# Turning the FFNs' token-major tall-set tiles with VectorE block transposes and ScalarE band copies instead of TensorE transposes, with six temporaries instead of nine

## The chip, the cores and the metric

The kernel runs on one core of one Trainium2 chip. The metric is the device time of one execution in microseconds (us), the median of several runs. TensorE (PE) multiplies matrices, VectorE (DVE) and ScalarE (ACT) work on tiles elementwise, GpSimd (POOL) issues only DMAs here, and SyncE (SP) issues the weight loads. Each engine runs its own instructions in order; they meet at semaphores.

## The reference, cut to what matters

One block of a model with 512 tokens of width 1024, in fp32: a feed-forward network (FFN), a mixer (short convolution and gated linear attention), a second FFN, and a last norm. The change touches the two FFNs only.

```
def swiglu(x, w_gu, w_down):                       # x: 512 x 1024, w_gu: 1024 x 5632
    g, u = jnp.split(x @ w_gu, 2, axis=-1)         # g, u: 512 x 2816
    return (jax.nn.silu(g) * u) @ w_down           # w_down: 2816 x 1024

x = x + 0.5 * swiglu(rmsnorm(x, g1), ffn1_w_gu, ffn1_w_down)
x = x + hybrid_mixer(rmsnorm(x, gm), ...)
x = x + 0.5 * swiglu(rmsnorm(x, g2), ffn2_w_gu, ffn2_w_down)
return rmsnorm(x, gf)
```

## The kernel before, in words

**Products.** Every fp32 product is made of three passes: each operand is split into a rounded high part and a remainder, and PE adds high x high, high x low and low x high. For weights, ACT casts the loaded tile `f` to `wh` (line 382) and DVE forms `wl = f - wh` (line 383). Activations are split the same way into `op` tiles (lines 673 and 674). There are three `wh` and three `wl` buffers, and a weight step is cast two steps ahead of the step that PE works on (`W.take`, `W.issue`).

**Seven products for eight.** Most large products are done by a Strassen-like scheme with seven block products, called m1, p2, q6, p5, q7, p3 and p4. It needs sums of weight blocks (accumulating DMAs on POOL, line 349, and a DVE subtraction for q7, line 376) and sums of operand blocks (lines 653 to 660).

**Tall sets.** The hidden width is 2816 = 22 tiles of 128, held in `hid` as [128 partitions, 22 tiles, 512 tokens]: hidden unit on the partitions, token along the row. Most of `hid` is made by *tall sets* (`up_tall`), each of four tiles starting at tile `f`. FFN 1 has four of them (f = 4, 8, 12, 16) and FFN 2 five (f = 0, 6, 10, 14, 18); the other tiles come from one ordinary set in each FFN, and from a plain start in FFN 1. A tall set has 14 steps: each of the seven products in two halves of the contraction. One step is 12 matmuls of 128x128 by 128x512 (line 701) and one pair `wh`, `wl`. In a tall set the activations are the stationary operand, so its results come out *token-major*: token on the partitions, hidden unit along the row, in PSUM banks `mm`. ACT and DVE combine them in temporaries `tp` of 128x512 (allocated with `T()`): g for the first 256 tokens after m1, p2 and p4, u after p5 and q7, and the second 256 tokens after q6 and p3. At the end of a set four `tp` tiles hold silu(g)·u for the four blocks of 128 tokens.

**The turn.** Since `hid` must have the hidden unit on the partitions, each set's four tiles are turned during the set behind it. `turn(f, js)` does two of the four `hid` tiles: for each it lets PE make four 128x128 fp32 transposes against `ident` into a PSUM tile `aux` (line 845) and ACT copies `aux` to `hid` (line 847). It is called twice for every set, by hooks after the next set's last m1 step and after the first half of its second product.

**What sets the order.** PE's order is the order in which the code is written (`manual_schedule`). The other engines' instructions are placed by a scheduler from the written order and its own estimates. Tile pools track reuse: a `tp` tile is given again when all its readers are done. In FFN 2 the hooks of the tall sets also hold the transposes of `X` (`natural`, line 1069) and, from the last set (f = 18) on, the splits of `hid` for the down projection (`make`).

Of the kernel before, what the change touches and what calls it, by code (L numbers as in the profile page):

```python
# [15 lines left out]
P = 128  # L16
S = 512
# [10 lines left out]
NTB = S // P  # L28
# [77 lines left out]
STEPS = []  # L106
# [28 lines left out]
TALL = {}  # L135
# [44 lines left out]
UPS = {}  # L180
# [54 lines left out]
def block_kernel(ctx: ExitStack, tc: tile.TileContext, xT, vecs, gf, gup, wgl, wts, out):  # L235
    nc = tc.nc
# [12 lines left out]
    def phase(odd, **bufs):  # L249

        stack = ExitStack()
        for n, b in bufs.items():
            pools[n] = stack.enter_context(
                tc.tile_pool(name=n if n != "small" else odd, bufs=b, reuse_waits="tile"))
        return stack

    def tile_of(pool, shape, dtype=F32):
        cnt[0] += 1
        return pools[pool].tile(shape, dtype, tag=pool, name=f"{pool}{cnt[0]}")

    def T(dtype=F32):
        return tile_of("tp", [P, S], dtype)
# [5 lines left out]
    def AUX():  # L268
        cnt[0] += 1
        return pa.tile([P, S], F32, tag="aux", name=f"aux{cnt[0]}")  # L270
# [133 lines left out]
    W = Weights(2)  # L404

    ident = front.tile([P, P], F32, tag="ident", name="ident")
# [180 lines left out]
    def mul(out_, a, b, eng=None):  # L587
        (eng or nc.vector).tensor_tensor(out=out_, in0=a, in1=b, op=ALU.mult)
# [201 lines left out]
    def ffn(up, down, norm, nxt, plain, at):  # L790
        hid = tile_of("hid", [P, KF, S])
        xo = begin_plain(up, hid, norm, plain, at) if plain else begin_weighed(hid, norm)

        def root(t):
            return 1.0 if plain else norm.r[t]

        def minus(t):
            return -1.0 if plain else norm.minus[t]

        done_tiles = {}  # L800

        def up_tall(f):
            g, u = {}, {}

            def done(p, banks):
                for t in range(2):
                    b = banks[t]
                    if p == "m1":
                        g[t] = T()
                        nc.scalar.copy(g[t], b)  # L810
                    if p == "p2":
                        nc.vector.tensor_tensor(out=g[t], in0=b, in1=g[t], op=ALU.add)
                        nc.scalar.activation(g[t], g[t], AF.Silu, scale=root(t))
                    if p == "p5":
                        u[t] = T()
                        nc.scalar.activation(u[t], b, AF.Copy, scale=-1.0)
                    if p == "q6":
                        g[2 + t] = T()
                        nc.scalar.copy(g[2 + t], b)  # L819
                    if p == "q7":  # L820
                        nc.vector.scalar_tensor_tensor(out=u[t], in0=b, scalar=-1.0, in1=u[t],
                                                       op0=ALU.mult, op1=ALU.add)
                    if p == "p3":
                        nc.vector.tensor_tensor(out=g[2 + t], in0=b, in1=g[2 + t], op=ALU.add)
                        nc.scalar.activation(g[2 + t], g[2 + t], AF.Silu, scale=root(2 + t))
                        if plain:
                            mul(u[t], u[t], g[2 + t])
                        else:
                            nc.vector.scalar_tensor_tensor(
                                out=u[t], in0=u[t], scalar=root(2 + t), in1=g[2 + t],  # L830
                                op0=ALU.mult, op1=ALU.mult)
                    if p == "p4":
                        nc.vector.scalar_tensor_tensor(out=g[t], in0=b, scalar=minus(t),
                                                       in1=g[t], op0=ALU.mult, op1=ALU.mult)
                if p == "p4":
                    done_tiles[f] = [g[0], g[1], u[0], u[1]]

            return Tall(xo, done)

        def turn(f, js):  # L840

            for j in js:
                o = AUX()
                for t in range(NTB):
                    nc.tensor.transpose(o[:, t * P : (t + 1) * P],  # L845
                                        done_tiles[f][t][:, j * P : (j + 1) * P], ident)
                nc.scalar.copy(hid[:, f + j], o)

        def up_set(i):
            f = [f for kind, f in UPS[up] if kind == "set"][i]  # L850
# [26 lines left out]
        def turn_pair(f):  # L877

            for j in range(2):
                o = AUX()  # L880
                for t in range(NTB):
                    c = (t % 2) * HW + j * P
                    nc.tensor.transpose(o[:, t * P : (t + 1) * P], narrow[t // 2][:, c : c + P],
                                        ident)
                nc.scalar.copy(hid[:, f + j], o)
# [39 lines left out]
        def at_step(key, f):  # L925
            hooks.setdefault(key, []).append(f)
# [27 lines left out]
        def begin(i):  # L954
            kind, f = UPS[up][i]
            return [((up, f), 1, "m1"), ((up, f), 0, ORDERS[up, f][1])] if kind == "tall" else \
                [(0, "q6"), (0, "p5")]

        if not plain:
            at_step(((up, UPS[up][0][1]), 1, "p5"), norm.finish)  # L960
        count = 0
        for i, (kind, f) in enumerate(UPS[up]):
            if kind == "set":
                if not plain:
                    at_step(begin(i + 1)[0], lambda f=f: turn_pair(f))
                continue
            keys = (begin(i + 1) if i + 1 < len(UPS[up]) else
                    [((down, 0), 1, "m1"), ((down, 0), 0, "p2")])
            for key, js in zip(keys, ((0, 1), (2, 3))):
                at_step(key, lambda f=f, js=js: turn(f, js))  # L970
            if nxt is None and i > 0:
                for p in ("p5", "q7"):
                    at_step(((up, f), 1, p), lambda i=count: natural(i))
                    count += 1
        hls = []
        if nxt is None:
            f = UPS[up][-1][1]
# [22 lines left out]
        def all_banks():  # L1000
            return [AUX(), AUX()] + [MM() for _ in range(KD - 2)]
# [15 lines left out]
        o = all_banks()  # L1017
# [36 lines left out]
        o = all_banks()  # L1054
# [9 lines left out]
    def natural(i):  # L1064

        X = XS[-1]
        o = AUX()
        for t in range(NTB):
            nc.tensor.transpose(o[:, t * P : (t + 1) * P], X[:, i, t * P : (t + 1) * P], ident)
        nc.scalar.copy(X[:, i], o)  # L1070
# [676 lines left out]
        for d, o in [(d, mm_single("w_o", KD, d * P, m_h, m_l)) for d in range(KD - 2, KD)]:  # L1747
            evac(d, o)

    FFN = dict(hid=1, tp=9)  # L1750
    with phase("small1", **FFN):
        W.phase(1)
        n1 = Norm(V_G1)
        for k in range(KD):
            nc.sync.dma_start(x[k], xT[k])
            if k == 0:
                with tc.manual_schedule(engines={ENG.DVE}):
                    n1.part(0, sooner=True)
                    W.issue()
            if k == 1 or k == 3:  # L1760
                W.issue()
        W.early = 5
        for k in range(KD):
            n1.add(k)
        nm = Norm(V_GM)
        ffn("ffn1_w_gu", "ffn1_w_down", n1, nm, PLAIN1, 5)
    with phase("small2", v=4, qk=2, g=1, y=1, small=1, tp=6):
        W.phase(4, 5)
        n2 = Columns(V_G2)
        mixer(nm, n2)  # L1770
    with phase("small3", **FFN):
        W.phase(5)
        ffn("ffn2_w_gu", "ffn2_w_down", n2, None, PLAIN2, 5)
# [43 lines left out]
```

## Time and profile before

| | |
|---|---|
| time, median of 3 runs | 1166.73 us (1166.69 to 1167.82) |
| span of the profiled execution, first to last instruction | 1165.7 us |
| PE busy | 1158.1 us (99%), 6428 matmuls |
| DVE busy | 895.6 us (77%) |
| ACT busy | 658.1 us (56%) |
| POOL busy | 127.3 us (11%) |
| mean granted TensorE clock | 0.999 |

The time of the profiled execution by itself is not given; its span is 1.0 us below the median time, which is taken as what lies around the span. Busy time is the union of an engine's instructions. Matmuls overlap in the records: each lasts longer than the distance to the next one, so a matmul's cost on PE's path is read from starts, or from the chain of work that ended last, and not from its mean duration.

### The profile page before, as it was taken

To read this page: it belongs to the slowest core of one execution; us is meant where nothing else is said; L and a number is where in the kernel's file an instruction comes from. 1 tells how busy PE (TensorE), PEld (TensorE's weight loads), DVE (VectorE), ACT (ScalarE), POOL (GpSimd) and SP (SyncE) were. 2 spreads that over 40 slices of the span, in tenths; PEclk is the share of its full clock that TensorE was granted. 3 is DMA by queue.
4 is the path that set the end of the run, shared out by engine and by line. 5 is a ranking of instruction groups with operands and counts; after the bars stand their busy time and mean duration, and the time that the engine had idled before them with its cause. 6 is when DMAs were issued, how large, how long until landed. Compare 5 with 4: busy or idle time off the path is not lost.

```text
span 1165.7 us, 16523 instructions
## 1 busy us (share of the span) xinstructions
PE 1158.1 (99%) x6428; PEld 1010.7 (87%) x6428; DVE 895.6 (77%) x1066; ACT 658.1 (56%) x832; POOL 127.3 (11%) x167
## 2 busy tenths in 40 slices
PE   9999999999999999999999999999999999999997
PEld 8888888989988888889999998888888888888886
DVE  7985666889887976777797999556876666799966
ACT  6565555634452756575655577525755556575543
POOL 0101110001120110111110111000111101101100
PEclk9999999999999999999999999999999999999999
DMA  9577786657665485878576787834567877877711
GB/s 365 130 187 163 167 219 163 174 131 174 170 206 152 99 220 155 219 198 216 134 175 163 177 215 213 287 104 126 118 181 163 219 181 163 210 168 173 184 41 73
DMA packets 59870, 203.22 MB, mean 174 GB/s; under 512 B 6960, under 2 KB 7088, under 8 KB 59792
## 3 DMA queue, kind: packets, MB, share of 16 engines
q0 software_dynamic: 20288, 73.41, 33.5%
q1 hardware_dynamic: 36912, 124.27, 32.7%
q10 hardware_dynamic: 2592, 4.49, 1.0%
q8 instruction: 50, 0.82, 0.3%
q14 instruction: 28, 0.23, 0.1%
HBM read 124.55 MB, written 8.39 MB: 114 GB/s over the span
## 4 chain that ended last, share of the span: by engine, by line
PE 99%; DVE 1%; ACT 0%; issue 0%; POOL 0%; POOLq 0%
PE mm L701 49%; PE mm L618 24%; PE mm L437 6%; PE mm L415 3%; PE mm L414 3%; PE mm L413 3%; PE aux L845 1%; PE mm L456 1%; PE mm L455 1%; PE mm L454 1%; PE mm L1088 1%; PE mm L1086 1%; PE mm L1087 1%; PE aux L1432 1%; PE aux L1435 0%; PE aux L1415 0%
## 5 line engine op out<-in xcount | busy, mean ns | idle before, releaser
L382 ACT CAST wh<-f 128x1024 fp32r<-128x1024 f32 (+1 forms) x349 | 365.2, 1048 | 358.7 <-PE mm L701 135.8
L383 DVE TENSOR_TENSOR wl<-f,wh 128x1024 fp32r<-128x1024 f32 (+1 forms) x349 | 424.6, 1218 | 177.0 <-ACT wh L382 176.1
L701 PE MATMUL mm<-wh,op 128*128 128x512 f32 x1680 | 528.3, 391 | 0.0
L701 PEld LDWEIGHTS mm<-wh,op 128*128 128x128 f32 x1680 | 315.4, 188 | 65.6 <-ACT tp L819 0.8
L701 PE MATMUL mm<-wl,op 128*128 128x512 f32 x840 | 327.3, 390 | 0.1
L618 PE MATMUL mm<-op,wh 128*128 128x256 f32 x1456 | 263.5, 284 | 0.0
L618 PEld LDWEIGHTS mm<-op,wh 128*128 128x128 f32 x1456 | 227.3, 192 | 0.7
L349 POOL DMA_DIRECT2D f<-f x132 | 113.8, 862 | 907.6 <-DVE wl L383 336.8
L618 PE MATMUL mm<-op,wl 128*128 128x256 f32 x728 | 206.0, 283 | 0.0
L701 PEld LDWEIGHTS mm<-wl,op 128*128 128x128 f32 x840 | 157.8, 188 | 32.5 <-DVE wl L383 0.9
L618 PEld LDWEIGHTS mm<-op,wl 128*128 128x128 f32 x728 | 139.4, 191 | 0.0
L673 ACT CAST op<-hid 128x1024 fp32r<-128x1024 f32 x42 | 44.0, 1050 | 22.5 <-PE mm L701 11.2
L674 DVE TENSOR_TENSOR op<-hid,op 128x1024 fp32r<-128x1024 f32 x42 | 51.2, 1220 | 3.0 <-ACT op L673 2.9
L413 PE MATMUL mm<-op,wh 128*128 128x512 f32 x132 | 51.4, 389 | 0.0
L414 PE MATMUL mm<-op,wh 128*128 128x512 f32 x132 | 51.4, 389 | 0.0
L415 PE MATMUL mm<-op,wl 128*128 128x512 f32 x132 | 51.4, 389 | 0.0
L437 PE MATMUL mm<-op,wh 128*128 128x512 f32 x192 | 48.2, 392 | 0.0
L376 DVE TENSOR_TENSOR f<-f,f 128x1024 f32<-128x1024 f32 x30 | 36.6, 1221 | 12.4 <-DMA f<-f 10.2
L437 PEld LDWEIGHTS mm<-op,wh 128*128 128x128 f32 x192 | 35.7, 188 | 8.0 <-ACT wh L382 0.5
L413 PEld LDWEIGHTS mm<-op,wh 128*128 128x128 f32 x132 | 24.8, 188 | 5.2
L414 PEld LDWEIGHTS mm<-op,wh 128*128 128x128 f32 x132 | 24.8, 188 | 5.2
L415 PEld LDWEIGHTS mm<-op,wl 128*128 128x128 f32 x132 | 24.8, 188 | 5.1
(326 smaller groups left out, 1196.4 us busy)
## 6 DMA issues: line engine op xcount, KB each, us to landing
f<-wts SPq DMA_DIRECT2D x219, 512.0 KB, 4.3
f<-f POOLq DMA_DIRECT2D x132, 512.0 KB, 5.2
X<-xT SPq DMA_DIRECT2D x8, 256.0 KB, 5.7
xs<-X POOLq DMA_DIRECT2D x8, 256.0 KB, 2.8
ga<-tp ACTq DMA_DIRECT2D x8, 256.0 KB, 5.2
gb<-tp ACTq DMA_DIRECT2D x8, 256.0 KB, 4.1
tp<-ga SPq DMA_DIRECT2D x8, 256.0 KB, 4.5
X<-xs POOLq DMA_DIRECT2D x8, 256.0 KB, 7.3
```

What stands on the lines that cost most here:

```text
L349: nc.gpsimd.dma_start(out_, a, accum_op=ALU.add)
L376: nc.vector.tensor_tensor(out=a11, in0=a11, in1=a22, op=ALU.subtract)
L382: nc.scalar.copy(h[:, :w], raw[:, :w])
L383: nc.vector.tensor_tensor(out=l[:, :w], in0=raw[:, :w], in1=h[:, :w].bitcast(F32), op=ALU.subtract)
L413: nc.tensor.matmul(o, wh, ah, start=first, stop=False)
L414: nc.tensor.matmul(o, wh, al, start=False, stop=False)
L415: nc.tensor.matmul(o, wl, ah, start=False, stop=last)
L437: nc.tensor.matmul(o[c], w[:, s : s + P], a[k], start=k == 0 and j == 0, stop=k == kt - 1 and j == 2)
L618: nc.tensor.matmul(to, ww[:, s], aa[:, t], start=fresh and k == 0 and e == 0 and j == 0, stop=k == 3 and j == 2, skip_group_check=True)
L673: nc.scalar.copy(hv, v)
L674: nc.vector.tensor_tensor(out=lv, in0=v, in1=hv.bitcast(F32), op=ALU.subtract)
L701: nc.tensor.matmul(self.bank[b][e], aa[:, c], ww, start=fresh and i == 0 and n == 0, stop=k == 3 and n == 2, skip_group_check=True)
```

## The change

In a tall set, when a pair of final tiles is ready (u after p3, g after p4), DVE transposes each of them blockwise, every 32x32 block by itself, into a new tile `z` of [128, 4 token blocks, 512]. In `z` the values inside a block are where they belong, and the blocks are still in the wrong partition bands. ACT puts them right: `move` copies, for each of the 4 source bands and 4 destination bands of 32 partitions, 32 partitions x 512 values from `z` to `hid`; that is 16 copies for a set. They are hooked onto the 12 steps behind the set (`after`), spread evenly. PE makes no transposes for the tall sets any more. The pool of `tp` tiles has six buffers instead of nine, and there is one `z` buffer, of the size of four `tp` tiles.

```diff
                 if p == "p4":
                     ...
+                if p == "p3":
+                    zs[f] = tile_of("z", [P, NTB, S])
+                    for t in range(2):
+                        block_turn(zs[f], 2 + t, u[t])
                 if p == "p4":
-                    done_tiles[f] = [g[0], g[1], u[0], u[1]]
+                    for t in range(2):
+                        block_turn(zs[f], t, g[t])
 
-        def turn(f, js):
-            for j in js:
-                o = AUX()
-                for t in range(NTB):
-                    nc.tensor.transpose(o[:, t * P : (t + 1) * P],
-                                        done_tiles[f][t][:, j * P : (j + 1) * P], ident)
-                nc.scalar.copy(hid[:, f + j], o)
+        def block_turn(z, at, v):
+            nc.vector.transpose(z[:, at], v)
+
+        def move(z, f, a, q):
+            src = z[32 * a : 32 * (a + 1)].rearrange("p t (b r) -> p b t r", r=P)
+            dst = hid[32 * q : 32 * (q + 1), f : f + 4].rearrange("p b (t r) -> p b t r", r=P)
+            nc.scalar.copy(dst[:, :, :, 32 * a : 32 * (a + 1)], src[:, :, :, 32 * q : 32 * (q + 1)])
 ...
+        def after(i):
+            seq, n = [], W.taken
+            while STEPS[n][1] is not None:
+                seq.append(STEPS[n])
+                n += 1
+            ups = [j for j, (n_, _) in enumerate(seq)
+                   if n_ in TALL and TALL[n_][0] == (up, UPS[up][i][1])]
+            at = max(ups) + 1
+            keys = []
+            for n_, p_ in seq[at : at + 12]:
+                keys.append((*TALL[n_], p_) if n_ in TALL else (0, p_))
+            return keys
 ...
-            keys = (begin(i + 1) if i + 1 < len(UPS[up]) else
-                    [((down, 0), 1, "m1"), ((down, 0), 0, "p2")])
-            for key, js in zip(keys, ((0, 1), (2, 3))):
-                at_step(key, lambda f=f, js=js: turn(f, js))
+            quads = [(a, q) for a in range(4) for q in range(4)]
+            keys = after(i)
+            for n, (a, q) in enumerate(quads):
+                at_step(keys[n * len(keys) // 16], lambda f=f, a=a, q=q: move(zs[f], f, a, q))
 ...
-    FFN = dict(hid=1, tp=9)
+    FFN = dict(hid=1, tp=6, z=1)
```

How the instructions stand on the engines, at three places. Names are those of the tiles, `out<-in`, with the size written; `x3` means three in a row. Lines of the changed kernel are some 20 higher than those of before from here on.

**ScalarE, first steps of FFN 1's third tall set (f = 12).** Line 810 evacuates m1, line 813 is the silu after p2. Before:

```order
L382 CAST wh_1463<-f_1362 128x1024
L810 COPY tp_1480<-mm_1444 128x512
L810 COPY tp_1482<-mm_1445 128x512
L847 COPY hid_193<-aux_1484 128x512
L847 COPY hid_193<-aux_1490 128x512
L382 CAST wh_1498<-f_1318 128x1024
L382 CAST wh_1526<-f_1360 128x1024
L847 COPY hid_193<-aux_1514 128x512
L847 COPY hid_193<-aux_1520 128x512
L382 CAST wh_1554<-f_1322 128x1024
```

After, at the same place:

```order
L382 CAST wh_1467<-f_1357 128x1024
L853 COPY hid_196<-z_1403 32x16x32 x3
L810 COPY tp_1484<-mm_1446 128x512
L810 COPY tp_1486<-mm_1447 128x512
L382 CAST wh_1491<-f_1310 128x1024
L853 COPY hid_196<-z_1403 32x16x32 x2
L382 CAST wh_1508<-f_1355 128x1024
L853 COPY hid_196<-z_1403 32x16x32 x4
L382 CAST wh_1538<-f_1314 128x1024
```

Three band copies now stand ahead of m1's evacuations, two and four ahead of the two following weight casts, where two pairs of copies from PSUM stood.

**VectorE, the same place.** Line 833 makes the last g tiles of the set before (f = 8), line 376 is the weight subtraction for q7, line 812 the addition after p2. Before:

```order
L833 SCALAR_TENSOR_TENSOR tp_1178<-mm_1141,tp_1178 128x512
L383 TENSOR_TENSOR wl_1447<-f_1320,wh_1446 128x1024
L383 TENSOR_TENSOR wl_1464<-f_1362,wh_1463 128x1024
L383 TENSOR_TENSOR wl_1499<-f_1318,wh_1498 128x1024
L376 TENSOR_TENSOR f_1318<-f_1318,f_1324 128x1024
L383 TENSOR_TENSOR wl_1527<-f_1360,wh_1526 128x1024
L376 TENSOR_TENSOR f_1360<-f_1360,f_1366 128x1024
L812 TENSOR_TENSOR tp_1480<-mm_1496,tp_1480 128x512
L812 TENSOR_TENSOR tp_1482<-mm_1497,tp_1482 128x512
L383 TENSOR_TENSOR wl_1555<-f_1322,wh_1554 128x1024
```

After:

```order
L833 SCALAR_TENSOR_TENSOR tp_1185<-mm_1146,tp_1185 128x512
L847 STREAM_TRANSPOSE z_1403<-tp_1183 128x512
L847 STREAM_TRANSPOSE z_1403<-tp_1185 128x512
L383 TENSOR_TENSOR wl_1449<-f_1312,wh_1448 128x1024
L383 TENSOR_TENSOR wl_1468<-f_1357,wh_1467 128x1024
L383 TENSOR_TENSOR wl_1492<-f_1310,wh_1491 128x1024
L376 TENSOR_TENSOR f_1310<-f_1310,f_1316 128x1024
L383 TENSOR_TENSOR wl_1509<-f_1355,wh_1508 128x1024
L812 TENSOR_TENSOR tp_1484<-mm_1489,tp_1484 128x512
L812 TENSOR_TENSOR tp_1486<-mm_1490,tp_1486 128x512
L376 TENSOR_TENSOR f_1355<-f_1355,f_1361 128x1024
L383 TENSOR_TENSOR wl_1539<-f_1314,wh_1538 128x1024
```

Two block transposes are put in behind line 833, and the second subtraction of line 376 has moved behind the two additions of line 812.

**VectorE, end of the last tall set of FFN 2 (f = 18).** Line 824 is the addition after p3, line 829 makes u, line 833 g; the next `wl` belong to the first steps of the down projection. Before:

```order
L824 TENSOR_TENSOR tp_9380<-mm_9242,tp_9380 128x512
L824 TENSOR_TENSOR tp_9382<-mm_9243,tp_9382 128x512
L674 TENSOR_TENSOR op_9532<-hid_7635,op_9531 128x1024
L829 SCALAR_TENSOR_TENSOR tp_9290<-tp_9290,col_7770,tp_9380 128x512
L829 SCALAR_TENSOR_TENSOR tp_9292<-tp_9292,col_7770,tp_9382 128x512
L383 TENSOR_TENSOR wl_9495<-f_9389,wh_9494 128x1024
L383 TENSOR_TENSOR wl_9513<-f_9442,wh_9512 128x1024
L833 SCALAR_TENSOR_TENSOR tp_9226<-mm_9192,col_7770,tp_9226 128x512
L833 SCALAR_TENSOR_TENSOR tp_9228<-mm_9193,col_7770,tp_9228 128x512
L383 TENSOR_TENSOR wl_9538<-f_9391,wh_9537 128x1024
```

After:

```order
L674 TENSOR_TENSOR op_9520<-hid_7630,op_9519 128x1024
L829 SCALAR_TENSOR_TENSOR tp_9261<-tp_9261,col_7765,tp_9357 128x512
L829 SCALAR_TENSOR_TENSOR tp_9263<-tp_9263,col_7765,tp_9359 128x512
L847 STREAM_TRANSPOSE z_9471<-tp_9261 128x512
L847 STREAM_TRANSPOSE z_9471<-tp_9263 128x512
L383 TENSOR_TENSOR wl_9481<-f_9367,wh_9480 128x1024
L383 TENSOR_TENSOR wl_9499<-f_9423,wh_9498 128x1024
L833 SCALAR_TENSOR_TENSOR tp_9219<-mm_9183,col_7765,tp_9219 128x512
L833 SCALAR_TENSOR_TENSOR tp_9221<-mm_9184,col_7765,tp_9221 128x512
L847 STREAM_TRANSPOSE z_9471<-tp_9219 128x512
L847 STREAM_TRANSPOSE z_9471<-tp_9221 128x512
L383 TENSOR_TENSOR wl_9526<-f_9369,wh_9525 128x1024
```

Two block transposes stand ahead of the `wl` of the down projection's first step, and two more ahead of its third. The order on POOL and SP is the same in both kernels.

More of the change, by code (lines that the diff above doesn't have):

```diff
@@ L798, in minus @@
             return -1.0 if plain else norm.minus[t]
-        done_tiles = {}
+        zs = {}
         def up_tall(f):
```

## The prediction

> **What bounds the kernel now.** I read the page's busy times, the chain that ended last, the groups, and then the chain in order of time around a turn.
>
> ```profile
> span 1165.7 us, 16523 instructions
> PE 1158.1 (99%) x6428; PEld 1010.7 (87%) x6428; DVE 895.6 (77%) x1066; ACT 658.1 (56%) x832; POOL 127.3 (11%) x167
> PE 99%; DVE 1%; ACT 0%; issue 0%; POOL 0%; POOLq 0%
> ...
> 133.37 0.87 PE aux L845 x8
> 134.24 2.75 PE mm L701 x12
> 136.99 0.87 PE aux L845 x8
> ```
>
> The chain runs on PE for 99% of the span, so a microsecond of PE's instruction stream is worth up to a microsecond of time, everywhere. The last three rows are the turn in the third tall set of FFN 1: eight transposes take 0.87 us of the chain, one weight step of 12 matmuls 2.75 us.
>
> **What is removed.** The groups, of which the first row has the times of the first and the last transpose:
>
> ```profile
> L845 PE MATMUL aux<-ident,tp x144: 270/272/273, 93.3 to 1058.2; 128*128 128x128 f32 x144
> ...
> L847 ACT COPY hid<-aux 128x512 f32<-128x512 f32 x36 | 19.3, 592 | 0.0
> ```
>
> There are 144 transposes, 18 groups of eight (two for each of nine tall sets): 18 x 0.87 = **15.7 us** off PE's path if nothing else comes late. One transpose lasts 272 ns, but they start every 0.87 / 8 = 0.109 us, and the starts are what counts. [...] ACT also loses 36 copies, 19.3 us.
>
> **What is added.** 36 block transposes of 128x512 on DVE, 144 band copies of 32 partitions x 512 values on ACT.
>
> ```profile
> L574 DVE STREAM_TRANSPOSE row<-tp x2: 712/712/712, 26.7 to 365.8; 128x512 f32<-128x512 f32 x2
> ...
> 133.88 1.08 ACT L847 COPY hid<-aux 128x512 f32<-128x512 f32 x2
> ...
> L673 ACT CAST op<-hid 128x1024 fp32r<-128x1024 f32 x42 | 44.0, 1050 | 22.5 <-PE mm L701 11.2 <-DVE hid L753 3.5 <-DVE hid L653 2.8
> ...
> L934 DVE SCALAR_TENSOR_TENSOR X<-mm,X 128x512 f32<-128x512 f32 x28 | 17.9, 682 | 0.0
> L812 DVE TENSOR_TENSOR tp<-mm,tp 128x512 f32<-128x512 f32 x18 | 11.6, 683 | 0.0
> ```
>
> The same block transpose, SBUF to SBUF, is in the trace at 0.71 us. A pair should take 1.3 (pairs of 128x512 operations overlap by about 0.1 on DVE, row of line 812 below), so a set costs DVE 2.6 us. No copy of 32 partitions with runs of 32 values is in the trace. Lower bound: 512 values for each partition like line 847, of which two take 1.08, 0.54 each. Upper bound: the 1.05 of a cast twice as wide. I take 0.54, as it is the nearest in length, and as the one strided pattern at hand costs nothing: line 934 (682 ns) writes `X` in runs of 128 values, line 812 (683 ns) whole rows. That is DVE and longer runs, so it is a choice and not a reading. A set costs ACT 16 x 0.54 = 8.6 us less four old copies, 2.1: net +6.5 us. PE gives back 1.74 us in a set.
>
> The stretches, each from one turn's end to the next one's; the third is the ordinary set and its neighbours at the end of FFN 1's up part, the last is the first part of the down projection in FFN 2:
>
> ```profile
> core 0: us, PE busy (x) PEld busy (x) DVE busy (x) ACT busy (x) POOL busy (x), PEclk, DMA share, GB/s
> 137.86:177.74 39.88, 39.88 (x185) 33.20 (x185) 25.43 (x26) 21.88 (x29) 5.22 (x7) 1.00 0.78 187
> 202.23:229.57 27.34, 27.34 (x210) 26.38 (x209) 23.12 (x25) 19.22 (x25) 1.72 (x2) 1.00 0.67 171
> 976.45:1017.30 40.85, 40.85 (x193) 33.98 (x193) 27.93 (x29) 24.23 (x32) 3.95 (x5) 1.00 0.70 184
> 1017.30:1058.48 41.18, 41.18 (x193) 33.84 (x193) 38.73 (x40) 28.72 (x36) 6.41 (x8) 1.00 0.78 171
> 1058.48:1099.26 40.78, 40.78 (x182) 33.75 (x181) 40.29 (x43) 22.87 (x25) 5.16 (x6) 1.00 0.78 189
> ```
>
> A middle tall set: PE 39.9 becomes 38.1; DVE 25.4 + 2.6 = 28.0; ACT 21.9 + 6.5 = 28.4. Both engines have 10 us of cover, so their work is hidden on the sum. The ordinary set: PE 27.3 - 1.7 = 25.6; ACT 19.2 + 6.5 = 25.7 would be full, but the order moves three operand casts of line 673 and one of line 990 (1.05 each) out of it, which makes some 21.5; DVE's 23.1 + 2.6 loses their partners too. I cost it at nothing; if the cover failed it would be 1.5 us. **The last two stretches have no cover on DVE:** 38.7 + 40.3 + 2.6 = 81.6 us of work in 41.18 + 40.78 - 1.74 = 80.2 us of PE.
>
> **The waits inside a middle set.** Sums hide two things, the queue on ACT and the accumulating DMAs. DVE, POOL and PE in the third tall set of FFN 1:
>
> ```profile
> 135.94 1.23 DVE L383 TENSOR_TENSOR wl<-f,wh 128x1024 fp32r<-128x1024 f32 x1 [2.96 <-ACT wh L382]
> 139.09 1.23 DVE L376 TENSOR_TENSOR f<-f,f 128x1024 f32<-128x1024 f32 x1 [1.92 <-DMA f<-f]
> 140.23 1.22 DVE L383 TENSOR_TENSOR wl<-f,wh 128x1024 fp32r<-128x1024 f32 x1
> 142.04 1.23 DVE L376 TENSOR_TENSOR f<-f,f 128x1024 f32<-128x1024 f32 x1 [0.59 <-DVE wl L383]
> 143.19 1.28 DVE L812 TENSOR_TENSOR tp<-mm,tp 128x512 f32<-128x512 f32 x2
> 144.38 1.22 DVE L383 TENSOR_TENSOR wl<-f,wh 128x1024 fp32r<-128x1024 f32 x1
> ...
> 133.06 0.86 POOL L349 DMA_DIRECT2D f<-f  x1 [1.41 <-DVE wl L383]
> ...
> 146.10 0.39 PE L701 MATMUL mm<-wl,op 128*128 128x512 f32 x1
> ```
>
> The `wl` made at 144.38 is ready at 145.60 and PE uses it at 146.10: a lead of 0.50 us. It is late because two subtractions of line 376 ahead of it wait for accumulations of POOL to land (the second had waited 0.59 us after its own predecessor had ended; its DMA was issued at 133.06, some 9 us earlier). These issues lie before the turn and do not move. PE, without two groups, wants that `wl` at 146.10 - 1.74 = 144.36. In the new order the pair of line 812 goes ahead of the second subtraction: cast 140.5 to 141.7, pair to 142.9, subtraction to 144.1, `wl` to 145.3, so PE waits 0.9 us. The same `wl` in FFN 1's fourth set, and in FFN 2's third:
>
> ```profile
> 183.26 1.22 DVE L383 TENSOR_TENSOR wl<-f,wh 128x1024 fp32r<-128x1024 f32 x1
> 185.98 0.39 PE L701 MATMUL mm<-wl,op 128*128 128x512 f32 x1
> ...
> 940.58 1.22 DVE L383 TENSOR_TENSOR wl<-f,wh 128x1024 fp32r<-128x1024 f32 x1
> 943.84 0.39 PE L701 MATMUL mm<-wl,op 128*128 128x512 f32 x1
> ```
>
> Leads of 1.50 and 2.04 us, so -0.24 and 0.30 once PE is 1.74 us earlier; the two block transposes ahead of p2's `wl` also start its accumulation up to 0.9 later. I put 0.5 us for the first, and 0.2 each for the second and the set behind it. Sum **1.8 us**. ACT's bursts come to 4 x 0.54 = 2.2 us ahead of one weight cast, in place of 1.08; a cast is made two steps ahead (5.5 us, less 1.05 for itself and 1.2 for `wl`: about 3 us of slack), so I cost the bursts at nothing, covered by that lead. The first three band copies wait for DVE's last block transposes, and m1's evacuations, the weight casts and through them DVE and PE queue behind; in a middle set DVE is done before ACT gets there, so nothing.
>
> **The end of FFN 2.** DVE's rows and the PE row that uses the first of the two casts:
>
> ```profile
> 1044.00 1.22 DVE L674 TENSOR_TENSOR op<-hid,op 128x1024 fp32r<-128x1024 f32 x1
> 1045.14 1.41 DVE L829 SCALAR_TENSOR_TENSOR tp<-tp,col,tp 128x512 f32<-128x512 f32 x2
> 1046.47 2.35 DVE L383 TENSOR_TENSOR wl<-f,wh 128x1024 fp32r<-128x1024 f32 x2
> 1048.74 1.40 DVE L833 SCALAR_TENSOR_TENSOR tp<-mm,col,tp 128x512 f32<-128x512 f32 x2
> 1050.39 1.23 DVE L383 TENSOR_TENSOR wl<-f,wh 128x1024 fp32r<-128x1024 f32 x1 [0.25 <-ACT wh L382]
> ...
> 1048.60 0.39 PE L701 MATMUL mm<-wl,op 128*128 128x512 f32 x1
> ```
>
> DVE works without a pause, and the first `wl` is ready at 1046.47 + 1.2 = 1047.7, a lead of 0.9. Two block transposes go ahead of it (1.3), while PE arrives 1.74 us earlier because the turn of the set before is gone: late by 0.9 - 1.3 - 1.74 = -2.1 us. Two more block transposes then meet PE again 1.74 us earlier, but the stall has already given DVE 2.1 us, and the idle 0.25 is used up; the rows behind have leads of 2 to 3 us against 3.0, so up to 0.7 more. I put **2.8 us**. Ends: 1.4 (81.6 - 80.2, everything else absorbed) and 4.4 (no lead used at all, both pairs and both groups of PE). The last set's own turn thus wins nothing.
>
> The six `tp` buffers cost nothing while a set needs six at a time (two each for g, u and the second g); they come free with DVE's block transposes, which the next m1 evacuation waits for already behind the first band copies. In the last part the tiles come again after several parts of 2.7 us.
>
> ```profile
> y<-tp SPq DMA_DIRECT2D x7, 256.0 KB, 2.1
> ```
>
> An output store is done in 2.1 us, which covers that; without it each part would wait a fraction of a microsecond.
>
> **Sum.** 15.7 - 1.8 - 2.8 = 11.1 us. The profiled span would be 1165.7 - 11.1 = 1154.6; the median lies 1.0 above it, so **1155.6 us** against 1166.7.
>
> **Rivals.**
>
> *All of it is won* (10%). If the accumulations land earlier as the set gets shorter and DVE finds room at the end, nothing is given back: 1166.7 - 15.7 = 1151.0. For it: the sums of the middle sets. Against it: the DVE sums of the last two stretches.
>
> *The accumulating DMAs set the pace* (9%). The row with a wait of 1.92 us and the DMA share of 0.70 to 0.78 speak for it: if landings keep their times in the seven sets that follow a turn inside a tall stretch, each gives back its 1.74 us, 12.2 us in all; with the end's 2.8 the gain is 0.7, so 1166.0, no change. Against it: the leads of 1.5 and 2.0 us in the other two sets shown.
>
> *ACT becomes the bound* (11%, slower). The mechanism is the price of a band copy. ACT's room in a middle set is 38.1 - 21.9 + 2.1 = 18.3 us, 1.15 us for each of 16 copies; and a burst of four at 1.05 makes 4.2 us ahead of a weight cast, over the 3 us of slack, with two more in the step before. At 1.05 us I reckon 2.2 us of stall in each of nine sets, 20 us: 1166.7 - 15.7 + 20 = 1171. It decides from a price of about 0.95 us on. For it: short runs and a quarter of the partitions are untried here. Against it: nothing in the trace shows a copy that pays by anything but its length. [...]
>
> *A transpose frees its whole duration* (1%): 144 x 0.272 = 39.2 us, so 1127.5 before any stall. The chain's 0.87 for eight is against it. [...]
>
> **How the numbers follow.** My forecast has 69%, with 1153 to 1160 as its own range: the end between 1.4 and 4.4, the middle sets between 0 and some 4 us. The range for 8 in 10 is 1152 to 1163: it leaves out most of "all won", the slower case and most of "no change". A difference of 0.2%, 2.3 us, is about what a measurement can tell from none. Faster: 69 + 10 + 1 and the small part of the DMA case with an earlier landing, 82%; same 7%; slower 11%.
>
> **What would show it.** Line 845 is gone and the nine tall stretches are shorter: right for the first step if the ones in the middle take 38.1 to 39.2 us. Band copies at 0.5 to 0.65 us and pairs of block transposes at 1.3 show the prices right; copies at 0.95 or more make the prediction wrong. PE's waits should stand at p5 of FFN 1's third set, for `wl` behind line 376, and at the first step of the down projection in FFN 2, behind the block transposes. If PE's waits are for `wh` behind band copies instead, ACT's bursts are what I left out.

## The result, and the profile after

The changed kernel takes **1162.03 us** (median of 4 runs, 1161.57 to 1162.50) against 1167.21 us for the kernel before on the same chip (4 runs, 1166.69 to 1167.82): a ratio of 0.9955, 95% interval 0.9941 to 0.9969. It is faster, by about 5.2 us and not by the 11.1 forecast. The spans of the profiled executions differ by 1165.7 - 1160.2 = 5.5 us. A single execution of one kernel below was slow, with 2963 us; it counts in that kernel's median and is not read further.

The page of the changed kernel (its last two rows are the chain's shares and the group of band copies), then the group of block transposes:

```profile
span 1160.2 us, 16386 instructions
PE 1145.0 (99%) x6284; PEld 995.4 (86%) x6284; DVE 912.6 (79%) x1102; ACT 726.9 (63%) x940; POOL 128.4 (11%) x167
PE 89%; ACT 4%; DVE 3%; DMA 2%; issue 1%; SPq 0%; ACTq 0%; POOLq 0%; DVEq 0%
...
L853 ACT COPY hid<-z 32x512 f32<-32x512 f32 x144 | 89.0, 618 | 5.4 <-DVE z L847 3.2
```

```profile
L847 DVE STREAM_TRANSPOSE z<-tp 128x512 f32<-128x512 f32 x36 | 23.3, 684 | 0.0
```

The 144 transposes are gone from PE. The chain that ended last is no longer PE throughout: PE holds 89% of it, where it had 99%, ScalarE now 4% and VectorE 3%. A band copy costs 618 ns.

PE's waits for other engines (columns: who waited for what, us in total, times, longest). Before, this view held one line, the 1.1 us for POOL's `ones` ahead of PE's first work, which every kernel has. The longest five now:

```profile
PE mm L701 <- ACT tp L819: 3.3, 1, 3.3
PE mm L701 <- DVE wl L383: 2.2, 3, 1.4
PE mm L618 <- DVE X L1029: 1.4, 1, 1.4
PE aux L279 <- POOL ones L276: 1.1, 1, 1.1
PE mm L618 <- DVE wl L383: 0.4, 1, 0.4
```

PE's starts in the two traces, compared one by one without the transposes, tell where each microsecond went:

| place in the changed kernel | us |
|---|---|
| 18 groups of transposes gone | -15.7 |
| first 13 us of the program | +1.1 |
| ordinary set and first part of FFN 1's down projection (218 to 248 us) | +2.55 |
| mixer and small differences | +0.35 |
| FFN 2, f = 14 (977 us) | +0.3 |
| FFN 2, f = 18, step q7 (1025 us) | +3.3 |
| first step of FFN 2's down projection (1043 us) | +0.9 |
| further into it (1066 us) | +1.5 |
| sum | -5.7 |

The sum is 0.2 from the 5.5 of the spans. The 1.1 us in the first 13 us is lost between matmuls there, and no edit explains it: PE's order in that part is unchanged, and in the traces of the eleven other kernels below PE stands between 0.4 us earlier and 0.5 us later at 20 us than in the kernel before. One trace does not show whether the other executions of the changed kernel have it.

The stretches (us, then busy time of PE, PEld, DVE, ACT, POOL): two middle sets of FFN 1, its ordinary set, the set f = 18 of FFN 2 and the start of its down projection.

```profile
97.00:135.00 38.00, 38.00 (x169) 31.37 (x168) 27.13 (x31) 29.54 (x41) 5.74 (x7) 1.00 0.79 197
135.00:173.00 38.00, 38.00 (x169) 31.34 (x168) 27.17 (x30) 29.55 (x40) 4.87 (x6) 1.00 0.77 194
...
202.00:227.00 25.00, 24.42 (x175) 22.86 (x174) 16.92 (x19) 21.26 (x29) 1.72 (x2) 1.00 0.57 147
...
997.20:1035.00 37.80, 34.47 (x156) 28.20 (x155) 32.95 (x34) 32.86 (x44) 3.90 (x5) 1.00 0.69 166
1035.00:1075.00 40.00, 38.05 (x167) 30.83 (x166) 38.48 (x44) 29.73 (x38) 5.16 (x6) 1.00 0.74 178
```

In the two middle sets of FFN 1 PE never pauses. In f = 18 it loses 3.3 us, though ACT and DVE are each busy for only 33 of 37.8: a sum again hides a queue. ACT's rows there, and the PE row that waits:

```profile
1015.93 1.05 ACT L673 CAST op<-hid 128x1024 fp32r<-128x1024 f32 x1
1017.00 1.88 ACT L853 COPY hid<-z 32x512 f32<-32x512 f32 x3
1018.90 1.34 ACT L813 ACTIVATE tp<-tp,col 128x512 f32<-128x512 f32 x2
1020.15 1.03 ACT L673 CAST op<-hid 128x1024 fp32r<-128x1024 f32 x1
1021.20 0.62 ACT L853 COPY hid<-z 32x512 f32<-32x512 f32 x1
1021.84 1.04 ACT L382 CAST wh<-f 128x1024 fp32r<-128x1024 f32 x1
1022.91 0.61 ACT L853 COPY hid<-z 32x512 f32<-32x512 f32 x1
1023.55 1.04 ACT L382 CAST wh<-f 128x1024 fp32r<-128x1024 f32 x1
1024.50 1.07 ACT L819 COPY tp<-mm 128x512 f32<-128x512 f32 x2
...
1025.13 0.50 PE L701 MATMUL mm<-wh,op 128*128 128x512 f32 x1 [3.33 <-ACT tp L819]
```

ACT works without a pause. Five band copies and two operand casts (line 673 serves the down projection, which starts only after this set) stand among the weight casts and ahead of line 819, the evacuation of q6's bank that q7 is to add into. By the trace that evacuation is what PE waits for last.

### The profile page after: what moved, and what is told of

Read it like the earlier page. It is cut to its first block, busy times and chain, and to the rows that moved or that the text cites. A ratio compares the mean times of both kernels' runs of the same rounds, so it can differ in the third digit from the quotient of the medians.

```text
span 1160.2 us, 16386 instructions
## 1 busy us (share of the span) xinstructions
PE 1145.0 (99%) x6284; PEld 995.4 (86%) x6284; DVE 912.6 (79%) x1102; ACT 726.9 (63%) x940; POOL 128.4 (11%) x167
## 4 chain that ended last, share of the span: by engine, by line
PE 89%; ACT 4%; DVE 3%; DMA 2%; issue 1%; SPq 0%; ACTq 0%; POOLq 0%; DVEq 0%
PE mm L701 44%; PE mm L618 23%; PE mm L437 5%; PE mm L415 2%; PE mm L414 2%; PE mm L413 2%; ACT hid L853 1%; DMA f<-f 1%; ACT wh L382 1%; PE mm L455 1%; PE mm L456 1%; PE mm L454 1%; DVE wl L383 1%; PE mm L1108 1%; PE mm L1107 1%
## 5 line engine op out<-in xcount | busy, mean ns | idle before, releaser
L618 PEld LDWEIGHTS mm<-op,wl 128*128 128x128 f32 x728 | 139.4, 191 | 0.6 <-DVE wl L383 0.6
L853 ACT COPY hid<-z 32x512 f32<-32x512 f32 x144 | 89.0, 618 | 5.4 <-DVE z L847 3.2
```

The lines of the kernel that those rows point to most:

```text
L618: nc.tensor.matmul(to, ww[:, s], aa[:, t], start=fresh and k == 0 and e == 0 and j == 0, stop=k == 3 and j == 2, skip_group_check=True)
L853: nc.scalar.copy(dst[:, :, :, 32 * a : 32 * (a + 1)], src[:, :, :, 32 * q : 32 * (q + 1)])
```

## The experiments

Theory A: PE waits behind the band copies in ScalarE's queue. Theory B, the prediction's own: VectorE, because of the block transposes. Theory C: six temporaries, or accumulating DMAs that keep their pace. A wait that is read off PE's starts below is the distance between two starts less the usual one; the views count only idle time, which is a little less.

**Which engine.** The band copies alone are made cheap, with the block transposes kept:

```diff
-            nc.scalar.copy(dst[:, :, :, 32 * a : 32 * (a + 1)], src[:, :, :, 32 * q : 32 * (q + 1)])
+            if q == 3:
+                nc.scalar.copy(hid[:, f + a].rearrange("p (t r) -> p t r", r=P),
+                               z[:, :, a * P : (a + 1) * P])
```

> All nine sets: VectorE's block transposes stay, but the 16 band copies of a set become four copies of 128 x 512 from z to hid that leave every block in its band (so hid holds the values in the wrong places). ScalarE then does as much for a turn as before the change (four copies of about 0.54 to 0.6 us), VectorE as much as after it. Theory A (ScalarE's queue): all waits behind band copies go, 2.55 + 0.34 + 5.65 = 8.5 us: 1153.5, between 1151.5 and 1155. Theory B (block transposes on VectorE, as in the prediction): the waits at FFN 2's end stay, 1159 to 1162. Theory C (temporaries or accumulating DMAs): 1162.

Measured: 1155.11 us (4 runs, 1153.96 to 1156.01), ratio 0.9892 (0.9879 to 0.9906). Its group of copies and PE's waits:

```profile
L852 ACT COPY hid<-z 128x512 f32<-128x512 f32 x36 | 20.5, 619 | 2.3 <-DVE z L847 2.3
```

```profile
PE mm L701 <- DVE wl L383: 2.7, 3, 1.6
```

The waits at 248, 1025 and 1066 us shrink from 1.55, 3.3 and 1.5 us to nothing, 0.4 and 0.3. So ScalarE's 68.5 us more of copies are the cause of most of what was given back, and theory B falls for these three. One wait does not move, 0.75 us at the first step of the down projection, released by a `wl` (line 383) right behind two block transposes:

```profile
1035.09 1.30 DVE L847 STREAM_TRANSPOSE z<-tp 128x512 f32<-128x512 f32 x2
1036.31 2.32 DVE L383 TENSOR_TENSOR wl<-f,wh 128x1024 fp32r<-128x1024 f32 x2
```

That one is theory B's, in the place that the prediction named. New here are 2.4 us near 893 us, behind an accumulating DMA: a first sight of what is late next.

The reverse, with copies kept and 28 of 36 block transposes left out:

```diff
-                    zs[f] = tile_of("z", [P, NTB, S])
-                    for t in range(2):
+                    zs[f] = zs[first] if zs else tile_of("z", [P, NTB, S])
+                    for t in range(2 if f == first else 0):
                         block_turn(zs[f], 2 + t, u[t])
```

> The reverse: ScalarE's 144 band copies stay, but only the first tall set of each FFN is block-transposed into z; the other seven sets copy from that z (their own results are not used). 28 of 36 block transposes (about 0.65 us each, 18 us of VectorE) are gone. Theory A (ScalarE's queue): the time stays within 1.5 us of 1162.0, and PE's gaps at 248, 1025, 1043 and 1066 us stay. Theory B (VectorE): about 1153.5. Theory C: 1162, as theory A; run e3 tells these two apart.

Measured: 1174.38 us (5 runs, 1171.64 to 1176.66), ratio 1.0058 (1.0044 to 1.0071): **slower than the kernel before**, which none of the theories said. Copies that wait for no block transpose were pulled forward by the scheduler, so that two sets' copies fall into one stretch (ACT's rows), and PE's waits are many:

```profile
117.39 1.89 ACT L854 COPY hid<-z 32x512 f32<-32x512 f32 x3
119.30 1.05 ACT L382 CAST wh<-f 128x1024 fp32r<-128x1024 f32 x1
120.38 2.50 ACT L854 COPY hid<-z 32x512 f32<-32x512 f32 x4
122.91 1.05 ACT L382 CAST wh<-f 128x1024 fp32r<-128x1024 f32 x1
123.98 1.87 ACT L854 COPY hid<-z 32x512 f32<-32x512 f32 x3
```

```profile
PE mm L701 <- DVE wl L383: 6.0, 15, 0.8
```

ACT has no room left, weight casts are late, the `wl` behind them too, and PE waits in the middle of sets where the changed kernel has no wait. It is no clean reverse, since the order moved. But VectorE's block transposes cannot be what made it slow, and the rival "ACT becomes the bound" is real once copies are packed more densely: from 97 to 135 us ACT is busy for 37.2 of 38.0 us, where it was 29.5 in the changed kernel.

**Which place.** Some sets are turned as before (`turn` and its hooks put back for them):

```diff
+        OLD = {"ffn1_w_gu": (16,), "ffn2_w_gu": (14, 18)}[up]     # all three places
...
+            if f in OLD:
+                for key, js in zip(keys, ((0, 1), (2, 3))):
+                    at_step(key, lambda f=f, js=js: turn(f, js))
```

> FFN 2's tall sets f = 14 and f = 18 are turned the old way (PE transposes, four ACT copies), the other seven the new way. After the change PE stood 3.4 us in the f = 18 set, 0.75 us at the first step of the down projection and 1.5 us further into it. Theory A, the band copies of these two sets fill ScalarE's queue: the three waits (5.7 us) go, and four groups of transposes (4 x 0.87 = 3.5 us) come back: 1162.0 - 2.2 = 1159.8 us, PE's start gaps above 0.4 us at the end of FFN 2 all but gone. Theory B, the block transposes of these two sets fill VectorE: the same 1159.8, since they are taken away too; this run only tells whether the place is right. Theory C, the waits come from the six temporaries or from accumulating DMAs that land at fixed times: the waits stay and the groups come back, 1165.5.

> FFN 1's last tall set (f = 16) alone is turned the old way, the other eight the new way. Theory A, its 16 band copies, put on the seven steps of the ordinary set, make the operand casts of the down projection late, and these the wait of 1.55 us at its first set and about 1.0 us before: 2.55 us go, two groups (1.7 us) come back: 1161.2, and no PE gap near 248 us. Theory B (block transposes on VectorE) says the same for this run. Theory C: the 2.55 us stay, 1163.8.

> FFN 1's f = 16 and FFN 2's f = 14 and f = 18 are turned the old way, the other six sets the new way. Theory A (ScalarE's queue in these three places): the waits at 248, 1025 and 1066 us go, and the one at the first step of the down projection too, since its block transposes are gone: 2.55 + 5.65 = 8.2 us back, six groups of transposes (5.2 us) paid: 1162.0 - 3.0 = 1159.0. Rival (the waits come from PE being early, whoever turns the tiles): the waits stay in size, 1165 or more.

Measured: with f = 14 and 18 of FFN 2 in the old way, 1161.11 us (four of its five executions from 1159.5 to 1163.2), ratio 0.9945 (0.9931 to 0.9958), against 1159.8 expected. That is faster than the kernel before and not to be told from the changed kernel; it has no trace that can be read, so its waits are not known. With f = 16 of FFN 1, 1164.32 us, ratio 0.9965 (0.9952 to 0.9979): the wait at 248 us is gone as expected, the 3.3 us at 1024 us stays. The time misses the expected 1161.2 by 3 us and comes near theory C's 1163.8, though theory C had the wait at 248 us stay; the profiled execution has some 1 us of new waits in FFN 2 and 3.2 us of matmuls at half rate behind two waits (granted clock 0.55 and 0.58, last section). With all three, **1159.58 us** (1158.41 to 1161.53), ratio 0.9940 (0.9927 to 0.9954), against 1159.0 expected: by its trace, six groups of transposes, 5.2 us, cost less than the waits that went with the copies in these three places. Of the waits 1.3 us and 0.25 are left, in f = 18, and the chain there (us, duration, what) begins with an accumulating DMA:

```profile
1009.37 9.07 DMA f<-f
1018.44 1.20 DVE tp L813 x2
1019.64 1.14 DVE f L376
```

**The temporaries.** Nine become six in the kernel before, nothing else: `FFN = dict(hid=1, tp=6)`.

> The kernel before with six temporaries in place of nine and nothing else. If the buffers cost nothing, as the prediction has it: no change, 1167.4 plus or minus 1.0 us on this chip. If the six buffers are part of what was not won: 1168.5 or more, with new PE gaps inside tall sets.

Measured: 1167.63 us (11 runs), ratio 1.0003 (0.9994 to 1.0012). No cost is seen, and by the interval it is at most 0.12%, 1.4 us; that part of theory C falls.

**Bursts or the sum.** First the last set's copies are hooked onto more steps:

```diff
-            for n_, p_ in seq[at : at + 12]:
+            for n_, p_ in seq[at : at + (18 if i + 1 == len(UPS[up]) else 12)]:
...
+            if plain and f == 16:
+                later.extend(quads[7:])      # nine copies behind the next four parts
+                quads = quads[:7]
```

> Every set is turned the new way, but the 16 band copies of the last set of each FFN are spread over more steps: in FFN 1 seven on the ordinary set and nine in the four parts behind it, in FFN 2 over 18 steps in place of 12. Theory A: the waits at 248 us (2.55 with what precedes it) and at 1066 us (1.5) shrink to a fifth, the one at 1025 us (3.4, from the set before) stays: 1162.0 - 3.3 = 1158.7. If it is the sum of ScalarE's work and not its bursts that costs, or the block transposes: no change, 1161 to 1163.

> As the run with spread copies, and FFN 2's f = 14 is turned the old way, so that no band copies fall into the last set. Theory A: the wait at 1025 us goes too (3.4 us back, two groups, 1.7 us, paid): 1157.0. If that wait is for the operands of the down projection alone, whatever the copies: it stays, 1160.5.

Measured: 1163.08 us (1161.33 to 1164.33) and 1163.69 us (1162.25 to 1165.11), where 1158.7 and 1157.0 were expected. Both missed, and the traces say why: the scheduler put the copies back nearly where they had been. In the changed kernel there are 3, 3, 2, 2 and 6 copies between casts from 1046.9 us on, in both kernels here 3, 2, 3, 1, 1 and 6, the last row in the first being

```profile
1060.23 3.77 ACT L853 COPY hid<-z 32x512 f32<-32x512 f32 x6
```

and in FFN 1 the last copy ends at 231 us, well ahead of the parts that it was meant to stand behind. The waits are back with them: in the first kernel 1.7 us at 247 us and 3.3 us at 1024 us, and the mean granted clock of its profiled execution is 0.997, the changed kernel's 0.999 (last section).

So the edit had hardly changed what it was to change. The next kernels hold each copy in its written order:

```diff
-            nc.scalar.copy(dst[...], src[...])
+            tc.keep_in_program_order(nc.scalar.copy(dst[...], src[...]))
```

> The changed kernel, but each band copy is held in the written order on ScalarE, so that the scheduler cannot pull copies forward into bursts ahead of weight and operand casts. Same copies, same block transposes, same steps. Theory A1 (the bursts and what stands behind them in ScalarE's queue cost, not the sum of the copies): in FFN 2's last set and in the down projection the copies come one or two at a time; the waits at 1025 and 1066 us shrink by two thirds, 3 us: 1159. In FFN 1's ordinary set a burst of six is left, so the wait at 248 us may stay. Theory A2 (the sum of ScalarE's work): no change, 1161 to 1163.

> Held in order, and the last set's copies of each FFN spread over more steps as in the run with spread copies, where the scheduler had pulled them forward again to the same places. Theory A1: the waits at 248 us and 1066 us are gone, the one at 1025 us shrinks to about 1.5 us (the run with three sets turned the old way keeps one of 1.55 there, behind an accumulating DMA): 1162.0 - 2.5 - 1.9 - 1.5 = 1156. Theory A2: 1161 to 1163.

> As the run before it, with FFN 2's f = 14 turned the old way. Theory A1: two groups, 1.74 us, are paid and no copy is left in the last set; since a wait of 1.55 us for an accumulating DMA stays there, nothing is won back for it: 1157.5. If copies in the last set still cost 3 us when held in order: 1154.5.

Measured: held, 1160.29 us (1159.77 to 1161.27), ratio 0.9940 (0.9928 to 0.9953); held and spread, **1159.96 us** (1159.64 to 1160.95), ratio 0.9938 (0.9926 to 0.9951); with f = 14 in the old way besides, 1160.36 us (1159.74 to 1161.49). Held and spread, the copies at the end of FFN 2 stand alone between casts:

```profile
1051.81 0.62 ACT L853 COPY hid<-z 32x512 f32<-32x512 f32 x1
1053.41 1.06 ACT L382 CAST wh<-f 128x1024 fp32r<-128x1024 f32 x1 [0.99 <-PE mm L701]
1054.49 0.62 ACT L853 COPY hid<-z 32x512 f32<-32x512 f32 x1
```

The wait at 248 us is gone (0.7 us are left at 220) and the one at 1066 is 0.25, with ACT as busy over the kernel as in the changed one, 729.1 us against 726.9. Held alone, with its burst of six and all 16 copies still in FFN 1's ordinary set, 0.9 us are left at 245 and 0.3 at 1066. So for these two places it is where the copies stand (A1) and not ACT's sum over the kernel (A2); at 1066 us that includes that only 11 of the 16 copies have run by then, where the changed kernel had run them all.

But 1159 and 1156 were expected. In f = 18 the wait did not shrink in either kernel; in the spread one it came apart into 1.15, 1.35 and 0.75 us between 1019 and 1025 us. Both also have waits that the changed kernel has not: by the view of PE's waits 1.5 us (held) and 1.0 us (held and spread) between 870 and 910 us, in FFN 2's first sets, and the spread one 1.0 us in the mixer, which the edit does not touch. In the chain to the last of the held one's waits there, at 899.7 us, an accumulating DMA, a silu and three band copies stand ahead of the weight cast, so the written order may well have a price of its own; no kernel here tests that. The third kernel has no copies in f = 18 and still waits 2.6 us there; its 1.6 us at 1066 stands behind 11 us in which VectorE works without a pause, so that place is not ScalarE's alone.

**What is late next.** The held and spread kernel's first wait in f = 18 begins with a subtraction that waits for an accumulation, and a weight cast that waits for the subtraction:

```profile
1017.07 1.23 DVE L376 TENSOR_TENSOR f<-f,f 128x1024 f32<-128x1024 f32 x1 [1.75 <-DMA f<-f]
...
1018.40 1.04 ACT L382 CAST wh<-f 128x1024 fp32r<-128x1024 f32 x1 [1.67 <-DVE f L376]
```

```diff
         def add(self, out_, a):
+            n = STEPS[self.issued][0]
+            if n in TALL and TALL[n][0] == ("ffn2_w_gu", 18):
+                return
             nc.gpsimd.dma_start(out_, a, accum_op=ALU.add)
```

> The kernel with copies held in order and spread, less the six accumulating DMAs of FFN 2's last set (its weight sums are left out, so the result differs; the subtraction of line 376 stays and takes the loaded blocks). The kernel it is taken from has waits of 1.4, 1.6 and 1.0 us between 1019 and 1025 us in that set, where line 376 stands 1.75 us behind a landing accumulation. Theory D (with the bursts gone, the landing of the accumulations is what PE waits for there): these waits go, 3.3 us, and the time falls to about 1157. If ScalarE's copies are still what makes PE wait there: the waits stay, 1160.

Measured: 1157.89 us (1157.45 to 1160.24), ratio 0.9924 (0.9910 to 0.9937), 2.1 us less by the medians, though the two ratios' intervals overlap; in the two traces 1.7 of 2.3 us of difference lie in this set. Of 3.25 us of waits there 1.7 are left, now behind ACT alone:

```profile
PE mm L704 <- ACT tp L822: 1.4, 2, 0.8
```

So in f = 18 of this kernel it is both, about half each: accumulations that land late, and copies, silus and weight casts ahead of the evacuations. Why the accumulations land late here is not shown.

Of the kernels that leave nothing out, the ones with three sets turned the old way and with copies held and spread are the fastest, 1159.6 and 1160.0 us. They lie about 2 us below the changed kernel's 1162.0; since their ratios to the kernel before have overlapping intervals with its own, that lead is likely rather than proven. What none of the edits reached is the 1155 that the turn would give with ScalarE's old load.

## Why the prediction was right or wrong

**Right:** the direction; 0.87 us for each group of transposes (in FFN 1's four sets PE came 5.9 us ahead, 4 x 1.74 less the 1.1 of the start); 1.3 us for a pair of block transposes (1.30 measured); the six temporaries at nothing; the middle stretches (14 steps of 2.72 us make 38.1).

**Wrong, and what the error rests on: "I cost the bursts at nothing, covered by that lead."** The 3 us of slack was reckoned for a weight cast alone. Where ACT also casts operands (FFN 1's ordinary set, FFN 2's f = 18, the down projection), the same queue holds line 673, silus and evacuations, and the lead is used up. Waits of 2.55, 3.3 and 1.5 us stand there, 7.35 of the 10 us given back; with cheap copies they were 0.7. At 248 and 1066 us it also helped to hold the copies apart. At 1025 us it did not, and with no copies left in that set 2.6 us still stood there, behind accumulations: in the changed kernel's trace ACT's queue is what PE waits for, but how much of the 3.3 us the copies cost by themselves stays open. The rule that the prediction wrote down for this case, waits "behind band copies", is what came, though at 1025 us PE waited not for `wh` but for an evacuation behind it in the same queue.

**The price of a band copy** was set at 0.54 and is 0.62. More than its length, the pairing was missed: three in a row take 1.88 us (row at 1017.00), so nothing overlaps, while three 128x512 copies of the same tile, 0.619 each alone, took 1.66 in the kernel with unmoved copies:

```profile
1041.38 1.66 ACT L852 COPY hid<-z 128x512 f32<-128x512 f32 x3
```

A set costs ACT 16 x 0.63 = 10 us, not 8.6. That the price "decides from about 0.95 us on" was too lax as well: in a middle set of the changed kernel one lead is nearly gone already,

```profile
147.70 1.23 DVE L383 TENSOR_TENSOR wl<-f,wh 128x1024 fp32r<-128x1024 f32 x1 [2.82 <-ACT wh L382]
```

ready at 148.93, used by PE at 149.08.

**The ordinary set**, "costed at nothing; if the cover failed 1.5 us": it failed, by 1.0 us in the set and 1.55 behind it. The operand casts were pushed back behind copies, so VectorE had six operand subtractions and four operand sums left from 228 us on, and the additions into `X` (line 1029) that free PE's banks came late behind the last of them:

```profile
242.49 2.35 DVE L674 TENSOR_TENSOR op<-hid,op 128x1024 fp32r<-128x1024 f32 x2
244.76 1.28 DVE L1029 SCALAR_TENSOR_TENSOR X<-aux,X 128x512 f32<-128x512 f32 x2
245.96 1.21 DVE L383 TENSOR_TENSOR wl<-f,wh 128x1024 fp32r<-128x1024 f32 x1
247.10 3.67 DVE L1029 SCALAR_TENSOR_TENSOR X<-mm,X 128x512 f32<-128x512 f32 x6
```

ACT's sum (21.3 of 25.0 us) was forecast rightly, 21.5, and said nothing of this.

**The waits inside middle sets**, 1.8 us: only 0.3 came, and none at p5 of FFN 1's third set. The term took the accumulations' landing as fixed. They landed sooner:

```profile
136.68 1.23 DVE L376 TENSOR_TENSOR f<-f,f 128x1024 f32<-128x1024 f32 x1 [0.53 <-DMA f<-f]
```

a wait of 0.53 for 1.92 before, and the second subtraction waited for none; the `wl` had a lead of 1.1 us.

**The end of FFN 2**, 2.8 us (1.4 to 4.4): 5.7 came, 3.3 in f = 18, 0.9 and 1.5. At the named place, the first step of the down projection, the mechanism held and the size did not: 0.9 for 2.1 (0.75 of it the wait, the rest a second start that comes 0.34 us after the first instead of 0.23). The lead of 0.9 less 1.3 is 0.4 late; the further 1.74 for "PE arrives earlier" should not have been added, because line 829 waits for a silu of PE's own results and so moves with PE:

```profile
1039.30 1.42 DVE L829 SCALAR_TENSOR_TENSOR tp<-tp,col,tp 128x512 f32<-128x512 f32 x2 [0.25 <-ACT tp L825]
```

With the 0.25 of this wait 0.65 of the 0.75 is found. The rest of the 5.7 came on ACT, which the term left out.

**The rivals.** "ACT becomes the bound, slower" did not come as a whole, but its mechanism stands behind most of the 10 us given back, and with copies packed more densely it gave 1174. "Accumulating DMAs set the pace" did not come in the changed kernel, which gained more than the 0.7 us of that rival; in the held and spread one accumulations were half of the wait in one set, f = 18.

## What to carry to other kernels

When work moves from the bound engine to one with room, compare it with the room in the queue at the places where that engine already serves several masters, not with the sum of a stretch: an in-order engine with 87% load can still hold the one evacuation that PE needs. Price a moved operation by its spacing in a row, not by a look-alike's paired time. And look at where the scheduler put an edited instruction before reading its result: two kernels here had their hooks changed, and the copies at the end of FFN 2 still stood 3, 2, 3, 1, 1 and 6 between casts in both.

## What the runs showed of the hardware that was not expected

After a wait of 3.33 us at the same step, PE came back at full clock in the changed kernel (1.00) and at about half in the one with f = 16 of FFN 1 in the old way (0.55; columns as above, PEclk third from the end). There most matmuls from 1024.86 to 1027.42 us start 0.43 us apart instead of 0.23, 1.6 us more in all. From 1068 us on the clock is low again, 0.58, behind 3.0 us in which PE was busy for 1.12. The changed kernel's rows, then the other's:

```profile
1021.00:1025.00 4.00, 0.80 (x4) 0.34 (x2) 3.53 (x4) 3.90 (x7) 0.00 (x0) 1.00 0.01 2
1025.10:1029.00 3.90, 3.87 (x17) 3.19 (x18) 3.90 (x4) 3.83 (x6) 0.00 (x0) 1.00 0.70 240
```

```profile
1021.00:1024.00 3.00, 0.00 (x0) 0.00 (x0) 2.52 (x4) 2.95 (x4) 0.00 (x0) 1.00 0.00 0
1024.20:1028.00 3.80, 3.73 (x9) 2.98 (x10) 3.80 (x4) 3.73 (x7) 0.00 (x0) 0.55 0.79 229
1065.00:1068.00 3.00, 1.12 (x5) 0.39 (x3) 3.00 (x4) 2.99 (x4) 0.86 (x1) 1.00 0.19 38
1068.00:1072.00 4.00, 4.00 (x11) 3.14 (x12) 4.00 (x5) 0.80 (x1) 0.00 (x0) 0.58 1.02 223
1072.00:1076.00 4.00, 4.00 (x19) 3.29 (x18) 3.05 (x5) 1.91 (x2) 0.00 (x0) 1.00 0.87 285
```

The view of PE's waits has none but the first above 1.6 us in that kernel, so the second drop did not need a wait of 3.3 us; and in the changed kernel a wait of 3.33 us was not enough for one. What decides is not shown.

The mean granted clock of whole executions varies too: 0.996 in four of the five of the kernel with f = 16 in the old way (1162.75 to 1165.05 us) and 0.998 in the fifth (1162.14 us), 0.997 to 0.999 in the four of the changed kernel. The profiled executions with spread copies and with block transposes left out have 0.997, the one with held copies 0.998. In the last, 21 matmuls from 1024.61 us on take 6.63 us of the chain, 0.32 each, and 62 from 1065.65 us on take 14.36, 0.23 each.

So in one of these runs 1.6 us more were lost behind a wait of 3.3 us. That may be part of why the executions of these kernels scatter by 1 to 5 us; with one trace for each kernel it is not shown.
